# Forty-eight weight tiles in a 512-column matmul form: GLU, part of the first MLP product, and the end of the scan's input and the keys

## The chip, the cores and the metric

The kernel runs on one core of one Trainium2 chip. The metric is the device time of one execution in microseconds (us). Before the change it is 1356.16 us, the median of 3 runs (1355.76 to 1356.31). "Within 0.2%" means within 2.7 us of that.

Engines are named as the profile names them: PE is TensorE's matmuls and PEld its weight loads, DVE is VectorE, ACT is ScalarE, POOL is GpSimd, SP is SyncE, whose queue issues most of the transfers.

## The reference

One decoder block, 256 positions of width 2048, everything in float32. A condition vector c makes six modulation rows (adaLN). A first norm and modulation give h. One product with `w_in` gives the input u of a state-space scan, the queries, keys and values of attention, and two gates. The two branches are gated, merged, projected and added to x; a second norm and modulation give h2, and an MLP with squared ReLU follows.

```python
c_act = jax.nn.silu(c)
mod = c_act @ w_ada[l] + b_ada[l]
h = rms_norm(x, norm_mix_g[l]) * (1.0 + sc1) + sh1
proj = h @ w_in[l]
u, q, k, v, ga, gb = jnp.split(proj, split_at, axis=-1)
...
    y = jax.nn.gelu(y).astype(u.dtype)
    return y * jax.nn.sigmoid(y @ w_glu + b_glu)
...
merged = (jax.nn.sigmoid(ga) * (y_ssm @ w_proj_ssm[l])
          + jax.nn.sigmoid(gb) * (y_att @ w_proj_attn[l]))
x = x + g1 * (merged @ w_out[l])
h2 = rms_norm(x, norm_mlp_g[l]) * (1.0 + sc2) + sh2
x = x + g2 * (jnp.square(jax.nn.relu(h2 @ w_ff1[l])) @ w_ff2[l])
return rms_norm(x, norm_final_g)
```

## The kernel before

**Products in three parts.** TensorE multiplies in a reduced float32 format (float32r). To keep the precision, every operand is split into a high part (rounded to float32r) and a low part (what is left), and a product is the sum of high x high, high x low and low x high. `split` (L179) does this for a weight tile: ACT casts `wraw` to `whi`, DVE subtracts to get `wlo`.

**Weight tiles.** All big products stream their weights through `stream` (L190) in tiles `wraw` of 128 partitions x 1024 columns (512 KB). There are seven buffers of `wraw` and four each of `whi` and `wlo`. A tile is either one row tile (128 rows) by 1024 columns or, where `kts` is given in pairs, two row tiles by 512 columns (`load`, L170).

**Three forms of a product.**

- `steps_t` (the "pt" form; `gemm_t` runs it): the weights are the stationary operand, h the moving one, and the result comes out transposed (columns of the weights on the partitions). For one weight tile it issues, for each of eight blocks of 128 columns, three matmuls of 256 columns (L270 high x high, L271 high x low, L272 low x high): 24 matmuls and 24 weight loads.
- `gemm_d` (the "pd" form, L279): the same product, but the high and the low part of h lie side by side, so that one matmul of 512 columns does high x high and high x low at once (L289), into the two halves of a PSUM bank; a matmul of 256 columns adds low x high to the second half (L293). A tile (two row tiles by 512 columns) has four blocks and two row tiles: 8 matmuls of 512 and 8 of 256 columns. The two halves of the bank have to be added when it is emptied. The result of one call is 512 columns wide, so 1024 columns take two calls ("halves" here, h = 0 and 1).
- `steps_n` (the "pn" form; `gemm_n`): h is stationary, the weights move, 12 matmuls of 512 columns for each tile (L327, L329, L331).

**PSUM banks.** `four` (L113) gives a product its four banks. As long as `turn` is None it takes them in turn from five ("mm"), so that a product finds one bank free and three that the product before has to release. From the MLP's second part on (`turn` is set to False at its start) products alternate between two sets. Three more banks ("ax") serve the small matmuls. `seeded` (L232) refills the banks with a partial sum before a product that continues an earlier one: one ACT copy for each bank, after the last cast of a weight tile emitted so far (`wcast`).

**Order.** Each engine runs its instructions in an order fixed when the program is built, by a planner that simulates the engines and takes what is ready by priority; loads and splits of weight tiles and the refills have a raised priority. `after(x)` adds an order behind instruction x.

**Lanes.** Between weight tiles, `step` runs small jobs from lanes. A lane has a rate: so many jobs for each tile. The lane "ada" makes the adaLN rows: each job loads a 512 KB tile of `w_ada` and multiplies and sums it on DVE (L391) one tile later. Its rate is set stage by stage by the constants R1 to R5, RS0 to RS3, RPA, RWO and RM. What is left of all lanes after the first part of the MLP is run at once by `flush` (L1677). The last jobs of that lane make the modulation of the last row tiles of h2. The lane "ssm" builds the scan's parameters on DVE.

**Stages.** The rows of h become ready in groups of 1, 3, 4 and 8 row tiles, so q, k, v, u and the first gate are computed in pieces that continue one another (`qkvu`; `duo` interleaves two). The last pieces come in this order: first gate and q interleaved, u (row tiles 8 to 15, L1337, about 186 to 212 us), `hop_in` (u is moved to another layout by 32 small transfers on POOL's queue), k (L1340, to 239 us), v (to 265 us; attention starts in it), then the rest of the gates beside attention and the scan. Then come one half of the attention projection, GLU (L1412, 451.5 to 474.6 us), the other half, the scan's projection, the merge, `w_out`, and the MLP.

**The MLP's first product** begins before all of h2 is known: for four units of 1024 columns (NP = 4) the row tiles that are ready are multiplied first and put into `part`. Unit 0 has four row tiles; units 1 to 3 have eight each (L1656, 647 to 718.5 us). `ff1` later adds the remaining row tiles with `gemm_d`.

## Time and profile before

| | us |
|---|---|
| median of 3 runs | 1356.16 |
| lowest, highest | 1355.76, 1356.31 |
| profiled execution | 1356.04 |
| its span, first to last instruction | 1354.3 |
| PE busy | 1342.8 |
| DVE busy | 1038.2 |
| ACT busy | 751.1 |
| POOL busy | 49.0 |

The profile is of one execution. Its page gives for each engine the busy time, a row of 40 equal slices of the span with the busy share in tenths, the clock granted to TensorE, the transfers, the chain of waits that ended last, and the costliest groups of instructions. A group line reads: source line, engine, operation, what it writes from what it reads, shapes, count, then busy us, the mean duration of one in ns, and the idle time of the engine before them with what ended it. A timeline line reads: start in us, duration in us, engine, source line, operation, and, in brackets, idle time of the engine before it. A line of the chain in order of time reads: start, duration, instruction, how many. A line of windows gives, for a stretch of the span, the busy time of each engine with the number of instructions, TensorE's granted clock, the busy share of the transfer engines, and GB/s. A matmul's duration runs from its start to its modelled end, and matmuls overlap.

### The profile page before, as it was taken

What the parts mean: (1) busy time and instruction counts of PE and PEld (TensorE: products, weight loads), DVE (VectorE), ACT (ScalarE), POOL (GpSimd) and SP (SyncE); (2) the same over time, 40 slices, a digit from 0 to 9 for tenths busy, and PEclk for the clock granted to TensorE, in tenths of its full rate; (3) what the DMA queues carried; (4) which work ended last, traced back from release to release, by engine and by line L of the source; (5) the groups of instructions that cost most, each with busy time, mean ns of one, the idle gap of its engine ahead of it and who ended that gap; (6) DMA issues with size and microseconds to landing.
All of it is one profiled execution on the core that took longest, in us unless ns stands there. A gap on an engine that the chain in (4) does not pass through costs nothing.

```text
span 1354.3 us, 21608 instructions
## 1 busy us (share of the span) xinstructions
PE 1342.8 (99%) x8276; PEld 1167.6 (86%) x8276; DVE 1038.2 (77%) x1441; ACT 751.1 (55%) x1045; POOL 49.0 (4%) x105
## 2 busy tenths in 40 slices
PE   9999999999999999999999999999999999999997
PEld 8898899788888988888998888888888888888886
DVE  7888998677987888988888967686765555565687
ACT  7768656766558543455546656353554544535544
POOL 0000004200004000000000000000000000000000
PEclk9999999999999999999999999999999999999999
DMA  9999977975568888997899897888878666566552
GB/s 377 407 408 409 389 252 210 306 241 180 159 215 262 314 283 300 334 337 290 291 342 339 296 235 263 220 281 258 276 243 230 190 187 197 187 188 198 176 196 83
DMA packets 116856, 357.09 MB, mean 264 GB/s; under 512 B 16728, under 2 KB 16864, under 8 KB 116464
## 3 DMA queue, kind: packets, MB, share of 16 engines
q1 hardware_dynamic: 113056, 348.83, 76.5%
q0 software_dynamic: 3120, 5.70, 1.4%
q8 instruction: 65, 1.06, 0.3%
q10 hardware_dynamic: 576, 1.18, 0.3%
q14 instruction: 39, 0.32, 0.1%
HBM read 350.79 MB, written 2.51 MB: 261 GB/s over the span
## 4 chain that ended last, share of the span: by engine, by line
PE 95%; ACT 2%; DMA 2%; DVE 1%; issue 0%; SPq 0%; ACTq 0%; DVEq 0%
PE pn L327 18%; PE pn L329 18%; PE pn L331 18%; PE pd L289 14%; PE pd L293 7%; PE pt L270 6%; PE pt L272 6%; PE pt L271 6%; DMA wraw<-in_w_in_dram 1%; PE ys L992 1%; ACT whi L184 1%; DMA xt<-in_xt_dram 0%; PE trh L834 0%; PE vr L954 0%; PE rk L794 0%
## 5 line engine op out<-in xcount | busy, mean ns | idle before, releaser
L186 DVE TENSOR_TENSOR wlo<-wraw,whi 128x1024 fp32r<-128x1024 f32 x448 | 546.2, 1224 | 254.4 <-ACT whi L184 253.0
L184 ACT CAST whi<-wraw 128x1024 fp32r<-128x1024 f32 (+1 forms) x449 | 467.3, 1051 | 479.6 <-PE pn L329 214.3
L289 PE MATMUL pd<-h2h,whi 128*128 128x512 f32 x800 | 207.3, 393 | 0.2 <-ACT whi L184 0.2
L327 PE MATMUL pn<-whi,ff 128*128 128x512 f32 x496 | 193.3, 390 | 0.0
L329 PE MATMUL pn<-whi,ff 128*128 128x512 f32 x496 | 193.3, 390 | 0.0
L331 PE MATMUL pn<-wlo,ff 128*128 128x512 f32 x496 | 190.9, 390 | 0.0
L289 PEld LDWEIGHTS pd<-h2h,whi 128*128 128x128 f32 x800 | 141.3, 189 | 22.9 <-ACT whi L184 0.4
L391 DVE SCALAR_TENSOR_TENSOR wraw<-wraw,cb 128x1024 f32<-128x1024 f32 x128 | 156.2, 1221 | 0.0
L327 PE MATMUL pn<-whi,ah 128*128 128x512 f32 x320 | 126.7, 400 | 0.8 <-ACT qk L1216 0.4
L329 PE MATMUL pn<-whi,ah 128*128 128x512 f32 x320 | 125.5, 392 | 0.0
L293 PEld LDWEIGHTS pd<-h2h,wlo 128*128 128x128 f32 x800 | 114.8, 190 | 11.5
L293 PE MATMUL pd<-h2h,wlo 128*128 128x256 f32 x800 | 117.9, 282 | 0.0
L331 PE MATMUL pn<-wlo,ah 128*128 128x512 f32 x320 | 115.9, 392 | 0.4 <-DVE wlo L186 0.4
L331 PEld LDWEIGHTS pn<-wlo,ff 128*128 128x128 f32 x496 | 93.1, 188 | 19.5
L329 PEld LDWEIGHTS pn<-whi,ff 128*128 128x128 f32 x496 | 93.2, 188 | 19.0
L327 PEld LDWEIGHTS pn<-whi,ff 128*128 128x128 f32 x496 | 93.1, 188 | 19.1
L270 PE MATMUL pt<-ah,whi 128*128 128x256 f32 x384 | 105.9, 286 | 0.2 <-DVE tz L611 0.2
L271 PE MATMUL pt<-ah,whi 128*128 128x256 f32 x384 | 104.9, 283 | 0.0
L272 PE MATMUL pt<-ah,wlo 128*128 128x256 f32 x384 | 95.9, 284 | 0.8 <-DVE wlo L186 0.7
L270 PEld LDWEIGHTS pt<-ah,whi 128*128 128x128 f32 x384 | 73.4, 192 | 1.8 <-ACT whi L184 0.7
L271 PEld LDWEIGHTS pt<-ah,whi 128*128 128x128 f32 x384 | 73.4, 192 | 0.2
L327 PEld LDWEIGHTS pn<-whi,ah 128*128 128x128 f32 x320 | 59.9, 188 | 15.3 <-ACT whi L184 1.3
(386 smaller groups left out, 2009.3 us busy)
## 6 DMA issues: line engine op xcount, KB each, us to landing
wraw<-in_w_ff_dram SPq DMA_DIRECT2D x256, 512.0 KB, 4.8
wraw<-in_w_in_dram SPq DMA_DIRECT2D x128, 512.0 KB, 6.1
wraw<-in_wat_dram SPq DMA_DIRECT2D x128, 512.0 KB, 5.9
ahm<-in_wat_dram SPq DMA_DIRECT2D x48, 512.0 KB, 10.2
wraw<-in_w_out_dram SPq DMA_DIRECT2D x32, 512.0 KB, 6.5
wraw<-in_w_proj_attn_dram SPq DMA_DIRECT2D x16, 512.0 KB, 5.7
wraw<-in_w_proj_ssm_dram SPq DMA_DIRECT2D x16, 512.0 KB, 6.4
ahm<-in_wan_dram SPq DMA_DIRECT2D x8, 512.0 KB, 10.6
```

Of the source, the lines that this page charges most:

```text
L184: h = self.nc.scalar.copy(hi[:, c], src[:, c])
L186: s = self.nc.vector.tensor_sub(lo, src, hi.bitcast(F32))
L270: nc.tensor.matmul(o, hi[:, c], xh[:, kx, :], start=st, stop=False, skip_group_check=True)
L271: nc.tensor.matmul(o, hi[:, c], xl[:, kx, :], start=False, stop=False, skip_group_check=True)
L272: self.mm = nc.tensor.matmul(o, lo[:, c], xh[:, kx, :], start=False, stop=sp, skip_group_check=True)
L289: nc.tensor.matmul(banks[blk], hi[:, cut(blk, k)], x2[:, ks[k], :, :], start=i + k == 0, stop=False, skip_group_check=True)
L293: self.mm = nc.tensor.matmul(banks[blk][:, S:2 * S], lo[:, cut(blk, k)], x2[:, ks[k], 0, :], start=False, stop=last and k == 1, skip_group ...
L327: nc.tensor.matmul(o, xh[:, kx, tk], hi[:, c], start=q == 0 and not full, stop=False, skip_group_check=full)
L329: nc.tensor.matmul(o, xl[:, kx, tk], hi[:, c], start=False, stop=False, skip_group_check=full)
L331: self.mm = last = nc.tensor.matmul(o, xh[:, kx, tk], lo[:, c], start=False, stop=q == n - 1, skip_group_check=full)
L391: v.scalar_tensor_tensor(w, w, 1.0, self.cb[:, (i % 2) * 1024:(i % 2 + 1) * 1024], op0=OP.mult, op1=OP.mult, accum_out=pc[:, i:i + 1])
L992: nc.tensor.matmul(p[q, c], self.cc[q, i, j].rearrange("p s c -> p (s c)"), self.sri[q, b % 2, i, c], start=i == 0, stop=False)
```

## The change

It moves 48 weight tiles from the pt form to the pd form: u's and k's last eight row tiles (8 tiles each), GLU (8) and units 1 to 3 of the MLP's first part (24). Each product of 1024 columns becomes two halves of 512.

- `gemm_d` takes a `seed`. The partial sum goes into the first half of each bank, and the second half is filled with zeros (ACT copies of the new column `zero`); the first matmul then accumulates.
- `join` empties a bank: ACT copies the second half, DVE adds the first half.
- `wide_last` replaces the last calls of `qkvu` for u and k. `duo` no longer prepares the first tile of u ahead (`prime`); v's is prepared in the second half of k.
- GLU: the split y lies as [row tile, high/low]; sigmoid, gating and split of the first four blocks follow the first half.
- The rates of the adaLN lane change in four places (R3, R4, RS0, RM).

```diff
-R3 = .25
-R4 = .7
+R3 = .15
+R4 = .8
 R5 = .9
-RS0 = .4
+RS0 = .55
...
-RM = 1.0
+RM = .8
...
-    def gemm_d(self, src, kts, c0, x2):
+    def gemm_d(self, src, kts, c0, x2, seed=None):
         nc = self.nc
         banks = self.four("pd")
+        full = self.seeded(banks, seed)
+        if full:
+            with self.tc.high_priority(offset=OFF), self.after(self.seedgate), self.after(self.wcast):
+                for o in banks:
+                    nc.scalar.copy(o[:, S:2 * S], self.zero.to_broadcast([P, S]))
...
-                nc.tensor.matmul(banks[blk], hi[:, cut(blk, k)], x2[:, ks[k], :, :], start=i + k == 0, stop=False,
+                nc.tensor.matmul(banks[blk], hi[:, cut(blk, k)], x2[:, ks[k], :, :], start=i + k == 0 and not full, stop=False,
                                  skip_group_check=True)
...
+    def join(self, banks, dests, view=lambda o: o):
+        for o, d in zip(banks, dests):
+            self.nc.scalar.copy(d, view(o[:, S:2 * S]))
+            self.nc.vector.tensor_add(d, d, view(o[:, 0:S]))
...
-        duo(order[12], order[13], (0,) * 8 + (1,) * 4 + (0,) * 4 + (1,) * 4, order[14])
-        qkvu(order[14])
+        duo(order[12], order[13], (0,) * 8 + (1,) * 4 + (0,) * 4 + (1,) * 4, None)
         self.want = lambda kt: None
+
+        def wide_last(which, after=None):
+            src, kts, c0 = place(which, 3, 3)
+            view = (lambda o: o.rearrange("p (c s) -> p s c", s=4)) if which == 3 else (lambda o: o)
+            for h in range(2):
+                dests = [self.uT[:, :, 4 * h + b, :] if which == 3 else self.qk[:, which, 4 * h + b, :] for b in range(4)]
+                seed = [lambda o, d=d: (view(o[:, 0:S]), d) for d in dests]
+                banks = self.gemm_d(src, kts, c0 + 512 * h, a2, seed)
+                if h and after:
+                    self.prime(*place(*after))
+                self.join(banks, dests, view)
+        wide_last(3)
         self.hop_in()
-        qkvu((1, 3, 3), (2, 3, 3))
+        wide_last(1, (2, 3, 3))
         self.lanes["ada"][1] = R4
...
-        yy = self.slot("VT", [P, 2, 8, S], F32R, name="yy")
+        yy = self.slot("VT", [P, 8, 2, S], F32R, name="yy")
...
-        banks = self.gemm_t(a["w_glu"][0], range(8), 0, yy[:, 0], yy[:, 1])
...
-        for b in range(4):
-            t = sg[:, b]
-            for k in range(2):
-                nc.scalar.activation(t[:, k], banks[b][:, k * S:(k + 1) * S], AF.Sigmoid,
-                                     bias=self.bglu[:, 2 * b + k:2 * b + k + 1])
-            s = slice(2 * b, 2 * b + 2)
-            v.tensor_mul(sc4(t), sc4(t), yT[:, s])
-            self.split(gg[:, 0, s], gg[:, 1, s], t)
+        for h in range(2):
+            banks = self.gemm_d(a["w_glu"][0], range(8), 512 * h, yy)
+            self.join(banks, [sg[:, 2 * h + b // 2, b % 2] for b in range(4)])
+            for b in (2 * h, 2 * h + 1):
+                t = sg[:, b]
+                for k in range(2):
+                    nc.scalar.activation(t[:, k], t[:, k], AF.Sigmoid, bias=self.bglu[:, 2 * b + k:2 * b + k + 1])
+                s = slice(2 * b, 2 * b + 2)
+                v.tensor_mul(sc4(t), sc4(t), yT[:, s])
+                self.split(gg[:, 0, s], gg[:, 1, s], t)
...
             if g:
-                banks = self.gemm_t(w1, range(0, 8), g * 1024, self.ah, self.al)
+                for h in range(2):
+                    self.join(self.gemm_d(w1, range(0, 8), g * 1024 + 512 * h, a2),
+                              [part[:, 2 * h + b // 2, (b % 2) * S:(b % 2 + 1) * S] for b in range(4)])
```

More of the change, by code (lines that the diff above doesn't have):

```diff
@@ L482, in consts @@
         nc.gpsimd.memset(self.mpos, MAGIC)
+        self.zero = self.col("zero", 1)
+        nc.gpsimd.memset(self.zero, 0.0)
         self.half = self.col("half", 1)
@@ L1318, in duo @@
             self.strict, self.seedgate = False, None
-            self.prime(*place(*after))
+            if after:
+                self.prime(*place(*after))
             evac(ub[0], banks[1], ub[1])
@@ L1335, in body @@
         qkvu(order[11], order[12], True)
-        duo(order[12], order[13], (0,) * 8 + (1,) * 4 + (0,) * 4 + (1,) * 4, order[14])
-        qkvu(order[14])
+        duo(order[12], order[13], (0,) * 8 + (1,) * 4 + (0,) * 4 + (1,) * 4, None)
         self.want = lambda kt: None
+        def wide_last(which, after=None):
[6 more added lines that the diff above has]
+                if h and after:
+                    self.prime(*place(*after))
+                self.join(banks, dests, view)
+        wide_last(3)
         self.hop_in()
-        qkvu((1, 3, 3), (2, 3, 3))
+        wide_last(1, (2, 3, 3))
         self.lanes["ada"][1] = R4
@@ L1408, in body @@
         for k in range(4):
-            self.split(sc4(yy[:, 0, 2 * k:2 * k + 2]), sc4(yy[:, 1, 2 * k:2 * k + 2]), yT[:, 2 * k:2 * k + 2])
+            self.split(sc4(yy[:, 2 * k:2 * k + 2, 0]), sc4(yy[:, 2 * k:2 * k + 2, 1]), yT[:, 2 * k:2 * k + 2])
         self.gate = self.hgate = None
         self.gates = [(None, None), self.done[-1]]
-        banks = self.gemm_t(a["w_glu"][0], range(8), 0, yy[:, 0], yy[:, 1])
         gg = self.slot("QT", [P, 2, 8, S], F32R, name="gg")
         sg = self.slot("S5", [P, 4, 2, S], name="sg")
-        for b in range(4):
-            t = sg[:, b]
-            for k in range(2):
-                nc.scalar.activation(t[:, k], banks[b][:, k * S:(k + 1) * S], AF.Sigmoid,
-                                     bias=self.bglu[:, 2 * b + k:2 * b + k + 1])
-            s = slice(2 * b, 2 * b + 2)
-            v.tensor_mul(sc4(t), sc4(t), yT[:, s])
-            self.split(gg[:, 0, s], gg[:, 1, s], t)
+        for h in range(2):
[8 more added lines that the diff above has]
+                self.split(gg[:, 0, s], gg[:, 1, s], t)
         proj_attn(1)
@@ L1556, in ff1 @@
                     else:
-                        nc.scalar.copy(q, banks[b][:, S:2 * S])
-                        v.tensor_add(q, q, banks[b][:, 0:S])
+                        self.join([banks[b]], [q])
                 self.flush("act")
@@ L1660, in body @@
                                     homes=[(wh[:, k, :], wl[:, k, :]) for k in range(4)])
-            for b in range(4):
-                if g:
-                    nc.scalar.copy(part[:, b, :], banks[b])
-                else:
+                for b in range(4):
                     with self.after(hs["h0"]):
```

## The prediction

> **What bounds the kernel now.** I read the profile's page first, then the chain of waits, then the timeline of the matmuls, because a busy matmul row says little about pace.
>
> ```profile
> span 1354.3 us, 21608 instructions
> PE 1342.8 (99%) x8276; PEld 1167.6 (86%) x8276; DVE 1038.2 (77%) x1441; ACT 751.1 (55%) x1045; POOL 49.0 (4%) x105
> PEclk9999999999999999999999999999999999999999
> PE 95%; ACT 2%; DMA 2%; DVE 1%; issue 0%; SPq 0%; ACTq 0%; DVEq 0%
> ```
>
> The chain that ended last is TensorE for 95% of the span, at full clock in every slice. So a stage gets shorter only where TensorE issues less work or issues it at a closer spacing. The profiled execution took 1356.04 us, 1.7 us more than its span and 0.1 us under the median of the runs shown (1356.16), so differences can be read against either.
>
> The groups give the old 256-column form and the new form's two parts these means:
>
> ```profile
> L270 PE MATMUL pt<-yy,whi 128*128 128x256 f32 x64 | 18.1, 283 | 0.0
> L289 PE MATMUL pd<-h2h,whi 128*128 128x512 f32 x800 | 207.3, 393 | 0.2 <-ACT whi L184 0.2
> L293 PE MATMUL pd<-h2h,wlo 128*128 128x256 f32 x800 | 117.9, 282 | 0.0
> ```
>
> By these means a weight tile (128 rows of 1024 columns) would cost 24 x 283 = 6.79 us in the old form (24 matmuls of 256 columns) and 8 x 393 + 8 x 282 = 5.40 us in the new one. That is a trap: the durations overlap. The timeline shows the starts. First and last matmuls of the GLU product (192 of them, old form), then three rows of the chain in order of time inside a later product that has the new form already:
>
> ```profile
> 451.52 0.28 PE L270 MATMUL pt<-yy,whi 128*128 128x256 f32 x1
> 451.64 0.28 PE L271 MATMUL pt<-yy,whi 128*128 128x256 f32 x1
> ...
> 474.56 0.40 PE L327 MATMUL pn<-whi,yh 128*128 128x512 f32 x1
> ```
>
> ```profile
> 952.88 1.84 PE pd L289 x8
> 954.72 0.95 PE pd L293 x8
> 955.67 1.84 PE pd L289 x8
> ```
>
> Old form: (474.56 - 451.52) / 192 = 0.120 us from start to start, so 24 x 0.120 = 2.88 us per weight tile. New form: 1.84 + 0.95 = 2.79 us per tile (0.230 per 512-column matmul, 0.119 per 256-column one). Both stream 6144 columns per tile; the new one saves eight matmul starts, and that is worth 0.09 us, not 1.4.
>
> **The change part by part.** *The saving.* Converted are 8 tiles of u, 8 of k, 8 of GLU and 24 of the MLP: 48 x 0.09 = 4.3 us of TensorE time, on the path everywhere.
>
> A page would make it less. The Trainium skill (TensorE: Matmul & The Clock Gate, section Back-to-back issue gap) gives N / 2.4 + 2.5 ns between matmuls of N columns; an estimate from that page is 2.62 us for an old tile and 2.60 for a new one, so 1.0 us for 48. The trace disagrees, with 2.88 and 2.79, and the sum goes by the trace.
>
> *Handing over the PSUM banks.* These products take four of five banks in turn. Today u, k, GLU and each MLP unit is one product; now each is two halves, so six hand-overs are new, and each finds one bank free and three that the half before has to release. In the last tile of a half a bank finishes every 0.70 us (2.79 / 4); the next half wants its banks 0.46 us apart (2 x 0.230). The fourth bank asked for was finished 0.70 us before the end and is wanted 1.38 us after it: 2.08 us. Emptying it now takes an ACT copy and a DVE add in place of one ACT copy; in u and k the refill with the earlier partial sum and a fill with zeros follow on ACT. Rows of the same shapes, and of DVE's usual work:
>
> ```profile
> L1557 ACT COPY fr<-pd 128x256 f32<-128x256 f32 x32 | 11.9, 373 | 10.0 <-PE pd L293 10.0
> L1558 DVE TENSOR_TENSOR fr<-fr,pd 128x256 f32<-128x256 f32 x32 | 13.2, 418 | 2.7 <-ACT fr L1557 1.9
> L237 ACT COPY pt<-qk 128x512 f32<-128x512 f32 x20 | 10.9, 601 | 0.0
> ...
> 703.30 1.22 DVE L186 TENSOR_TENSOR wlo<-wraw,whi 128x1024 fp32r<-128x1024 f32 x1
> 704.43 1.22 DVE L391 SCALAR_TENSOR_TENSOR wraw<-wraw,cb 128x1024 f32<-128x1024 f32 x1
> ```
>
> Without the refill: 0.37 + 0.42 = 0.79 us, plus whatever stands ahead on DVE, whose long pieces start 1.13 us apart. With one piece ahead it is 1.92 us, inside 2.08. With the refill (two more ACT pieces; the zero fill is shown nowhere, I bound it by 0.37 for a 256-column copy and 0.60 for a 512-column one, nearest the former) it is 0.79 + 0.74 + 1.13 = 2.66 us, 0.6 late. What such a hand-over costs TensorE today is seen where the last old-form MLP unit meets the first new-form product:
>
> ```profile
> 718.24 0.28 PE L272 MATMUL pt<-h2h,wlo 128*128 128x256 f32 x1
> 718.71 2.11 PE L289 MATMUL pd<-h2h,whi 128*128 128x512 f32 x8 [0.18 <-ACT whi L184]
> ...
> 949.95 1.98 PE L289 MATMUL pd<-h2h,whi 128*128 128x512 f32 x8
> ...
> 727.26 2.46 PE L289 MATMUL pd<-h2h,whi 128*128 128x512 f32 x10
> 729.56 0.40 PE L293 MATMUL pd<-h2h,wlo 128*128 128x256 f32 x2
> ```
>
> Its eight matmuls took 2.11 us, against 1.98 where banks are plentiful: 0.13 us. At 727.26 ten 512-column matmuls stand where a half's last tile has two before each pair of 256-column ones: eight of the following half were pulled ahead of a tile not ready yet: the order on TensorE is made round foreseeable waits, and the free bank offers 0.70 us of such work per tile in hand. I take 0.13 us for each of the six new hand-overs (0.8 us) and 0.15 us more for the three that refill (into u's second half and both halves of k): 0.45 us. Together 1.25 us; bounds are nothing and, with one long piece ahead everywhere, 3 x 0.6 + 0.8 = 2.6 us.
>
> *Vector and scalar work.* Added: 48 DVE adds, 48 ACT copies of 256 columns, and in u and k 16 refills and 16 zero fills in place of 8 refills of 512; 20 ACT copies of 512 go (4 each in u and k, 12 in the MLP; GLU's sigmoids read the banks themselves today). What is beside it:
>
> ```profile
> core 0: us, PE busy (x) PEld busy (x) DVE busy (x) ACT busy (x) POOL busy (x), PEclk, DMA share, GB/s
> 186.00:212.00 26.00, 26.00 (x365) 25.42 (x367) 23.62 (x28) 13.54 (x19) 0.00 (x0) 1.00 0.71 230
> 212.00:239.00 27.00, 27.00 (x311) 26.68 (x301) 23.85 (x29) 16.05 (x31) 17.97 (x37) 1.00 0.79 187
> 239.00:265.00 26.00, 26.00 (x125) 21.59 (x124) 15.64 (x27) 18.61 (x38) 5.84 (x11) 1.00 1.04 330
> 451.00:475.00 24.00, 24.00 (x198) 23.82 (x197) 20.65 (x29) 10.60 (x15) 0.00 (x0) 1.00 0.92 315
> 647.00:719.00 72.00, 71.82 (x600) 71.61 (x599) 60.63 (x88) 34.29 (x46) 0.00 (x0) 1.00 0.90 326
> ```
>
> In u and k (the first two rows) DVE has 47.5 us of work in 53. The 16 adds bring 5.3 to 6.7 (0.33 to 0.42 each, overlapped or not); R3 at .15 takes two adaLN pieces (1.22 each) out: 50.4 to 51.8 in 51.6 us. That is full. But the branch's parameter work in it isn't urgent, and the next stage has DVE at 15.64 of 26. Nothing, as long as the splits go first. GLU: 20.65 of 24 plus 2.6 to 3.4 is full too, with spill into the projection behind it. MLP: 60.6 - 5 x 1.22 + 24 x 0.33 to 0.42 = 62.4 to 64.6 of 69.9. ACT has room: 29.6 of 53 in u and k, and 48 x 0.37 - 16 x 0.60 = 8 more.
>
> *Rates and transfers.* I worked the adaLN lane's credits through tile by tile. In the last tiles of q, then u and k, it issues 3 jobs instead of 6; in v 7 instead of 5; in the first gate product 8 instead of 7; in the three MLP units 19 instead of 24, which leaves 5 for the flush behind them instead of 1. A job is 0.52 MB and 1.22 us of DVE. The third row is the tight one: transfers are full there (share 1.04), and one more job falls between k's last tile and v's last: 0.52 / 330 GB/s = 1.6 us. TensorE already starves there a little:
>
> ```profile
> 265.97 0.50 PE L327 MATMUL pn<-whi,ah 128*128 128x512 f32 x1 [0.29 <-ACT whi L184]
> 267.54 0.50 PE L331 MATMUL pn<-wlo,ah 128*128 128x512 f32 x1 [0.43 <-DVE wlo L186]
> ...
> L184 ACT CAST whi<-wraw 128x1024 fp32r<-128x1024 f32 x8 | 8.4, 1049 | 7.1 <-DMA wraw<-in_w_in_dram 5.5 <-PE pn L331 1.5
> ```
>
> I take nothing, since the code holds four split tiles ahead, with -0.7 us (these stalls gone) and +1.6 us as bounds. The four extra jobs of the flush are 4.9 us of DVE just before the last row tiles of h are needed, but five jobs fewer ran before them, so the sum of work ahead is the same: nothing, at most 4.9 less the 1.5 us that the order above leaves (727.26 to 729.1 is spent on other matmuls): 3.4 us. Weights now come as two row tiles of 512 columns; later products do so without starving: nothing. The new constant column on GpSimd: nothing. GLU's gating of its first four blocks moves beside the second half.
>
> **Sum.** -4.3 + 0.8 + 0.45 = -3.0 us: 1356.04 - 3.0 = 1353.0 us.
>
> **The rivals.** *A, no saving in the spacing.* Half a 512-column interval is 0.115 us, the lone 256-column one 0.119; if with h and yy the pair ran at 2 x 0.120, the 4.3 would go and 1.25 us stay: 1357.3. For it speaks the page's rule above, by which hardly anything is to be had; against it 800 matmuls at this pace on the same buffer layout. *B, the hand-overs take more.* One long DVE piece ahead everywhere and one more transfer late in v: -4.3 + 2.6 + 1.0 (between 0 and 1.6) = -0.7, 1355.3 us. For it: DVE is full in u, k and GLU. Against it: matmuls can be pulled forward. *C, slower, by DVE queueing before an add.* If not one but two long pieces stand ahead, the bank is released 0.79 + 2.26 = 3.05 us after it was finished, 1.0 late, and with a refill 1.7 late. Twelve hand-overs are open to it: the six new ones, and six that there are today but where the new form asks for its banks faster, or hands them on by an add (into GLU, from u to k, into each of the three MLP units, and behind the last of them). Three refill: 3 x 1.7 + 9 x 1.0 = 14 us, 1356.04 - 4.3 + 14 = 1365.8 if all are struck; half of them gives 1358.8. It decides from 7 us on, that is from half of them. For it: DVE in those stages is over 95% by the sums above. Against it: the hand-overs of today, beside a DVE at 85 to 90%, cost about 0.1 us each. *D, more than forecast:* free hand-overs and the v stalls gone: -4.3 - 0.7 = -5.0, 1351.0.
>
> **How the numbers follow.** About 0.2% (2.7 us) is what a measurement of this kernel can tell from no change. Forecast (1351.9 to 1354.2): 0.45. D: 0.12. B: 0.25. A: 0.05. C: 0.13. Of the forecast's 0.45 some 0.09 lies above 1353.4, within 0.2%. Faster by over 0.2%: 0.36 + 0.12 = 0.48; within: 0.09 + 0.25 + 0.05 = 0.39, slower 0.13. Range: from 1350.4 (D and its margin) to 1358.8 (half of C, over A and the late transfers).
>
> **What would show it.** Right: 512-column starts 0.230 us apart in u, k, GLU and MLP units; about 2.79 us per tile there; single gaps of some tenths of a us at the hand-overs. Wrong: spacing of 0.240 (A); TensorE waiting for the joining adds or for the refills by more than 0.5 us a time (B, C); waits for weight transfers in v, or for h's last row tiles after the flush. A result under 1350 would mean a stall in before that I have not seen.

## The result: 1.3% slower, and the profile after

| | before | after |
|---|---|---|
| median, same chip | 1356.24 us (4 runs, 1355.76 to 1358.42) | 1373.86 us (4 runs, 1371.93 to 1374.36) |
| ratio | | 1.0128, 95% interval 1.0113 to 1.0143 |
| profiled execution (span) | 1356.04 us (1354.3) | 1374.12 us (1372.3) |

The forecast was 1353.0 us and the range ended at 1358.8. From the page of after, in its order: span, engines, clock by slice, the chain that ended last, two groups.

```profile
span 1372.3 us, 20961 instructions
PE 1346.8 (98%) x7892; PEld 1147.2 (84%) x7892; DVE 1052.1 (77%) x1489; ACT 761.8 (56%) x1097; POOL 49.2 (4%) x106
PEclk9999999999999999999999999999999999999999
PE 86%; DVE 7%; ACT 3%; issue 2%; DMA 1%; DVEq 0%; ACTq 0%
L294 PE MATMUL pd<-h2h,whi 128*128 128x512 f32 x992 | 268.0, 394 | 3.8 <-ACT whi L184 2.5
L298 PE MATMUL pd<-h2h,wlo 128*128 128x256 f32 x992 | 156.1, 282 | 3.4 <-DVE wlo L186 3.4
```

384 matmuls fewer, and still TensorE is busy 4 us longer: a busy row says little about pace here as before. The chain tells more: TensorE held 95% of it, now 86%, and DVE went from 1% to 7%. The two groups now have idle time before them that ACT's casts and DVE's splits ended. To see in which stages the time went, I took the first matmul of each product from the timeline of after:

```profile
185.50 0.40 PE L294 MATMUL pd<-ah,whi 128*128 128x512 f32 x1
244.38 0.40 PE L337 MATMUL pn<-whi,ah 128*128 128x512 f32 x1
437.07 0.39 PE L337 MATMUL pn<-whi,yh 128*128 128x512 f32 x1
458.83 0.39 PE L294 MATMUL pd<-yy,whi 128*128 128x512 f32 x1
482.79 0.40 PE L337 MATMUL pn<-whi,yh 128*128 128x512 f32 x1
505.82 0.39 PE L337 MATMUL pn<-whi,gg 128*128 128x512 f32 x1
...
656.53 0.48 PE L294 MATMUL pd<-h2h,whi 128*128 128x512 f32 x1
792.72 0.40 PE L337 MATMUL pn<-whi,ff 128*128 128x512 f32 x1
```

In before, the starts that the prediction does not show (u, v, the first attention part, the scan's projection, the units, the product behind them):

```profile
185.80 0.28 PE L270 MATMUL pt<-ah,whi 128*128 128x256 f32 x1
238.81 0.48 PE L327 MATMUL pn<-whi,ah 128*128 128x512 f32 x1
429.76 0.39 PE L327 MATMUL pn<-whi,yh 128*128 128x512 f32 x1
496.34 0.39 PE L327 MATMUL pn<-whi,gg 128*128 128x512 f32 x1
647.02 0.36 PE L270 MATMUL pt<-h2h,whi 128*128 128x256 f32 x1
774.70 0.40 PE L327 MATMUL pn<-whi,ff 128*128 128x512 f32 x1
```

Differences of such starts give the stages:

| stage (first matmul to first matmul) | before | after |
|---|---|---|
| u and k | 53.02 | 58.88 |
| v and gates | 190.95 | 192.69 |
| GLU | 23.03 | 23.96 |
| second attention part of the projection | 21.79 | 23.03 |
| units 1 to 3 and the product behind them | 127.68 | 136.20 |

Together +18.3 us; the span is 18.0 longer, and all other stages agree within 0.3 us. Every edited stage lost, though by the saving alone each was to win 0.7 to 2.2 us.

What the units wait for, from the view of waits over 669 to 742 us (total, times, longest, us):

```profile
ACT whi L184 <- PE pd L294: 18.3, 3, 7.5
ACT whi L184 <- DMA wraw<-in_w_ff_dram: 16.1, 9, 9.6
DVE wlo L186 <- ACT whi L184: 11.9, 6, 3.8
PE pd L298 <- DVE wlo L186: 3.4, 6, 0.9
PE pd L294 <- ACT whi L184: 2.5, 3, 1.3
```

Read from below: TensorE waits for split weights, the splits for casts, and the casts for TensorE to let go of a buffer, or for loads that themselves were issued late. The four buffers of split weights come free late. The planned order of TensorE's built program (matmuls in a row on one bank and weight tile in one line, bank and tile numbers kept) says why:

```
2998 L294 MATMUL pd0_6752<-h2h_6464,whi_6758 128x512 x2
...
3003 L298 MATMUL pd0_6752<-h2h_6464,wlo_6759 128x256 x2
3004 L294 MATMUL pd0_6752<-h2h_6464,whi_6782 128x512 x2
...
3006 L294 MATMUL pd0_6752<-h2h_6464,whi_6807 128x512 x2
...
3008 L294 MATMUL pd0_6752<-h2h_6464,whi_6832 128x512 x2
3009 L294 MATMUL pd1_6753<-h2h_6464,whi_6758 128x512 x2
```

At a hand-over one bank of the five is free (6752). The planner fills it from all four weight tiles (6758, 6782, 6807, 6832) before the next bank is asked for. So every tile is held until the last bank has had it: four buffers fill together and come free together, and casts, splits and loads bunch behind them. This is the "0.70 us of such work per tile in hand" that the prediction counted as a protection.

### The profile page after: what moved, and what is told of

It reads as the page before. It is cut to its first block, busy times and chain, and to the rows that moved or that the text cites. A ratio compares the mean times of both kernels' runs of the same rounds, so it can differ in the third digit from the quotient of the medians.

```text
span 1372.3 us, 20961 instructions
## 1 busy us (share of the span) xinstructions
PE 1346.8 (98%) x7892; PEld 1147.2 (84%) x7892; DVE 1052.1 (77%) x1489; ACT 761.8 (56%) x1097; POOL 49.2 (4%) x106
## 4 chain that ended last, share of the span: by engine, by line
PE 86%; DVE 7%; ACT 3%; issue 2%; DMA 1%; DVEq 0%; ACTq 0%
PE pd L294 17%; PE pn L337 17%; PE pn L339 17%; PE pn L341 17%; PE pd L298 9%; PE pt L272 2%; PE pt L270 2%; PE pt L271 2%; DVE wraw L401 2%; DVE wlo L186 2%; DMA wraw<-in_w_ff_dram 1%; ACT whi L184 1%; ACT bp L776 1%; DVE rw L983 1%; PE rk L806 0%
## 5 line engine op out<-in xcount | busy, mean ns | idle before, releaser
L294 PE MATMUL pd<-h2h,whi 128*128 128x512 f32 x992 | 268.0, 394 | 3.8 <-ACT whi L184 2.5
L294 PEld LDWEIGHTS pd<-h2h,whi 128*128 128x128 f32 x992 | 170.7, 189 | 28.5 <-ACT whi L184 3.3
L298 PEld LDWEIGHTS pd<-h2h,wlo 128*128 128x128 f32 x992 | 149.4, 190 | 25.2 <-DVE wlo L186 6.5
L298 PE MATMUL pd<-h2h,wlo 128*128 128x256 f32 x992 | 156.1, 282 | 3.4 <-DVE wlo L186 3.4
L341 PE MATMUL pn<-wlo,ah 128*128 128x512 f32 x320 | 113.1, 396 | 2.0 <-DVE wlo L186 2.0
L337 PEld LDWEIGHTS pn<-whi,ah 128*128 128x128 f32 x320 | 60.3, 189 | 16.2 <-ACT v L1228 2.0
L341 PEld LDWEIGHTS pn<-wlo,ah 128*128 128x128 f32 x320 | 60.4, 189 | 14.8 <-DVE wlo L186 2.4
L339 PEld LDWEIGHTS pn<-whi,ah 128*128 128x128 f32 x320 | 60.4, 189 | 12.2
L270 PE MATMUL pt<-ah,whi 128*128 128x256 f32 x256 | 69.2, 285 | 0.2 <-DVE tz L623 0.2
L271 PE MATMUL pt<-ah,whi 128*128 128x256 f32 x256 | 68.7, 283 | 0.0
L272 PE MATMUL pt<-ah,wlo 128*128 128x256 f32 x256 | 60.2, 284 | 0.8 <-DVE wlo L186 0.7
```

Source lines behind the costliest of these rows:

```text
L270: nc.tensor.matmul(o, hi[:, c], xh[:, kx, :], start=st, stop=False, skip_group_check=True)
L271: nc.tensor.matmul(o, hi[:, c], xl[:, kx, :], start=False, stop=False, skip_group_check=True)
L272: self.mm = nc.tensor.matmul(o, lo[:, c], xh[:, kx, :], start=False, stop=sp, skip_group_check=True)
L294: nc.tensor.matmul(banks[blk], hi[:, cut(blk, k)], x2[:, ks[k], :, :], start=i + k == 0 and not full, stop=False, skip_group_check=True)
L298: self.mm = nc.tensor.matmul(banks[blk][:, S:2 * S], lo[:, cut(blk, k)], x2[:, ks[k], 0, :], start=False, stop=last and k == 1, skip_group ...
L337: nc.tensor.matmul(o, xh[:, kx, tk], hi[:, c], start=q == 0 and not full, stop=False, skip_group_check=full)
```

## The experiments

Stages as above ("u to gates" is u, k, v and gates; "GLU to scan" is GLU, the second attention part and the scan's projection, 45.43 in before), in us of the profiled execution. Where nothing is edited in "u to gates" and the rates are those of before, it still lies between 242.8 and 245.3, so differences of 1.5 us in that column are not read.

| run | median | ratio to before, 95% | u to gates | GLU to scan | units |
|---|---|---|---|---|---|
| before | 1355.75 to 1356.24 by job | 1 | 243.97 | 90.25 | 127.68 |
| after | 1373.86 | 1.0113 to 1.0143 | 251.57 | 92.42 | 136.20 |
| e1 units on two sets | 1366.68 | 1.0055 to 1.0088 | 251.61 | 93.17 | 129.75 |
| e2 old rates | 1372.92 | 1.0107 to 1.0137 | 249.69 | 92.81 | 136.23 |
| e3 new rates only | 1364.66 | 1.0046 to 1.0076 | 246.39 | 90.25 | 134.10 |
| e4 tile order | 1372.37 | 1.0102 to 1.0132 | 255.05 | 91.48 | 129.96 |
| e5 RM only | 1359.24 | 1.0016 to 1.0035 | 243.28 | 90.25 | 131.89 |
| e6 units alone, two sets | 1359.66 | 1.0019 to 1.0047 | 244.91 | 90.25 | 132.52 |
| e7 u and k alone | 1361.18 | 1.0023 to 1.0053 | 249.45 | 90.53 | 127.65 |
| e8 GLU alone | 1357.91 | 1.0007 to 1.0026 | 243.42 | 91.54 | 127.65 |
| e9 units mixed | 1356.19 | 0.9995 to 1.0013 | 243.27 | 90.25 | 129.00 |
| e10 units pinned | 1359.94 | 1.0019 to 1.0041 | 244.25 | 90.25 | 132.56 |
| e11 GLU, two sets | 1355.73 | 0.9989 to 1.0007 | 243.35 | 89.53 | 127.68 |
| e12 GLU and two units | 1355.23 | 0.9990 to 1.0007 | 242.82 | 89.53 | 126.74 |
| e13 u and k, no refill | 1358.91 | 1.0016 to 1.0036 | 246.74 | 90.25 | 127.66 |
| e14 the same, pinned | 1363.51 | 1.0039 to 1.0070 | 252.90 | 90.25 | 127.66 |
| e15 units, ACT release | 1358.50 | 1.0012 to 1.0034 | 244.48 | 90.25 | 128.40 |
| e16 the same, pinned | 1358.06 | 1.0009 to 1.0031 | 243.47 | 90.25 | 130.60 |
| e17 e16 and GLU | 1358.99 | 1.0014 to 1.0031 | 245.25 | 89.53 | 129.36 |

### Order, banks and rates: four changes to the pair

**e1**, after with the halves of the MLP units alternating between the two sets of PSUM banks:

```diff
                 self.lanes["ada"][1] = RM
                 self.agate = None
+                self.turn = False
```

> The changed kernel with one line more: from unit 1 of the MLP's first part on, the halves take their PSUM banks alternately from the two sets, so no half waits for the one before it. Theory O (order): with one free bank the planner runs a half block by block through all four of its weight tiles, so all four split buffers are needed at once and come free together; with banks at hand the order goes tile by tile, and the MLP units with the product behind them (656.5 to 792.9 us in the changed kernel, 136.4 us, against 127.8 before) shorten by 8 to 10 us: 1364 to 1366 us. Theory D (DVE load: 24 adds more and the splits late for that): the adds and the adaLN pieces stay, so the stretch stays within 2 us: 1372 to 1374. Theory R (the rates): the same as D.

**e2**, after with the four rates of before:

```diff
-R3 = .15
-R4 = .8
+R3 = .25
+R4 = .7
...
-RS0 = .55
+RS0 = .4
...
-RM = .8
+RM = 1.0
```

> The changed kernel with the four rates of before (R3 .25, R4 .7, RS0 .4, RM 1.0). Theory R: most of the loss is the rates, time 1358 or less. Theory O: the order block by block stays, so the converted stages stay long; only the single stalls in v (268.9 us) and beside the scan (377.2 us), 2 to 6 us with the clock's halving behind the latter, may go: 1367 to 1374. Theory D: more adaLN pieces in u, k and the MLP units on a DVE that is the bound: slower than the changed kernel, 1374 to 1380.

**e3**, before with the four rates of after (the diff reversed):

> The kernel of before with the four new rates alone. Theory R: slower by 3 us or more, with the stalls in v or beside the scan in it. Theories O and D: within 3 us of before (1353 to 1359), since no hand-over is new and DVE has no adds more.

**e4**, after with the matmuls of a weight tile ordered behind the last of the tile before, wherever halves share one set of banks:

```diff
+            turn = self.mm if i and self.turn is None else None
...
-                            f(blk, k)
+                            with self.after(turn):
+                                f(blk, k)
```

> The changed kernel, in which every matmul of a tile of a half is ordered behind the last matmul of the tile before it, wherever the banks come from one set (u, k, GLU, MLP units). The banks' hand-over, the adds, the rates are as in the changed kernel; only the order is tile by tile. Theory O in its strict form (the order does the harm, not the wait for the bank): the stalls of the converted stages fall from about 14 us to a few: 1360 to 1365. If the hand-over itself costs (each half waits 1 us for its banks): 1366 to 1372. Theory D: unchanged, 1372 to 1375.

Measured: in the units both e1 and e4 win back over 6 of the 8.5 us. In e1 no half waits for the banks of the half just before it; in e4 the banks are released as in after and only the order is forced. So in the units the order on the late banks makes most of the loss. Two rows for 669 to 700 us (busy time of PE, PEld, DVE, ACT, POOL, then the clock), after and e1:

```profile
669.00:700.00 31.00, 28.74 (x169) 24.39 (x168) 26.27 (x43) 15.65 (x28) 0.00 (x0) 1.00 0.89 306
```

```profile
669.00:700.00 31.00, 31.00 (x182) 27.32 (x181) 29.41 (x48) 15.67 (x25) 0.00 (x0) 1.00 1.00 361
```

With two sets TensorE does not pause in this stretch, DVE does 3 us more in the same time, and the same loads come at 361 GB/s instead of 306: DVE and the transfers were not full in after, they were waiting. What e1 still loses in the units it loses at their end, where transposes wait, as in e6 below. By its time e4 lies in theory D's range, but only because it loses in u and k what it wins in the units (66.36 us there, 58.88 in after): there the first matmuls of a half waited 5.13 us for the refilled bank, and the refill had waited for DVE's addition of the half before:

```profile
219.06 0.71 ACT L237 COPY pd<-qk 128x256 f32<-128x256 f32 x2 [5.54 <-DVE uT L313]
```

Undoing the rates changes the median by 0.9 us (e2), which the spread of the runs does not tell from nothing, yet alone they cost 8.7 us (e3, 1364.66 against 1355.96), 6.4 of them in the units. The loss of the rates and that of the form overlap; they do not add.

### The parts one by one, rates as in before

**e5**, before with one rate changed (the flush then holds five jobs; in before it holds one, not none as the expectation says):

```diff
-RM = 1.0
+RM = .8
```

> The kernel before with RM alone at .8, so that five adaLN jobs instead of none stand at the flush after the first MLP half's fourth unit; R3, R4 and RS0 stay. Theory F (the flush holds h's last row tiles back): the stages up to the MLP units as before (within 0.3 us each), units 1 to 3 with ff1(1,0) 131 to 134 us instead of 127.7 with the extra time between the flush and the first matmuls after it, the whole 1359 to 1362 us. Rival R (what the run with the new rates alone lost came of R3, R4 and RS0, which move jobs from v and the gates to later): units 127.7, the whole 1356 us.

**e6**, before with the units' part of the change alone and `self.turn = False` as in e1; **e7** with `wide_last` alone; **e8** with the GLU part alone (their diffs are the parts of the change's own).

> The kernel before with units 1 to 3 of the first MLP product in the 512-column form, their halves alternating between the two sets of PSUM banks; u, the keys, GLU and all rates as before. Theory O (the loss of the units comes of one free bank and an order block by block, and of the flush): with both gone the 24 tiles save 24 x 0.09 = 2.1 us: units and ff1(1,0) 125.2 to 126.2 us instead of 127.7, the whole 1353.5 to 1354.5 us. Rival Q (the form itself costs the units time, by its 32 DVE and ACT operations more): units 129 us or more, the whole 1357 us or more. Rival S (any new order costs some us somewhere): units 127.7 or less, but other stages longer.

> The kernel before with the last eight row tiles of u and the keys in the 512-column form and nothing else; rates as before. Theory U (the refills and zeroings by ACT and the sums by DVE come into a stretch in which both engines have the scan's setup to do; it costs by itself): u and k with v and the gates 248 to 252 us instead of 243.97, half-clock stretch near 240 us, the whole 1360 to 1364 us. Rival N (the loss there comes only with the other parts or the rates): 243.3 us, the whole 1355.5 us.

> The kernel before with GLU alone in the 512-column form; rates as before. Theory O: GLU 23.9 us instead of 23.03 and the second attention part of the projection 22.6 to 23.0 instead of 21.79, the whole 1357.7 to 1358.5 us. Rival N (those stalls come of what the other parts leave late): GLU 22.3 us, the projection 21.8, the whole 1355.5 us.

By its numbers e5 is as theory F expected: 4.2 us more in the units' stage, 1359.24 in all. The transposes of h's last row tiles (the tile view gives count, duration, first and last start) stand far ahead in before and at the very end in e5, before first:

```profile
L834 PE MATMUL trh<-ident,xs x13: 270/273/273, 694.2 to 707.7; 128*128 128x128 f32 x13
```

```profile
L834 PE MATMUL trh<-ident,xs x14: 272/273/328, 715.5 to 717.7; 128*128 128x128 f32 x14
```

In e5 TensorE had finished unit 3 by then and waited, 0.5 us between the transposes and 2.1 us for their results, and it ran at half clock for 3.4 us behind that (last section).

Theory F's reason does not hold, though. The column B of the modulation is the later of the two columns that a group of rows needs. It was done twice in this time, for row tiles 8 to 11 and for 12 to 15; before first, then e5:

```profile
675.16 0.16 DVE L1052 TENSOR_TENSOR B<-pcs,pack 128x4 f32<-128x4 f32 x1
...
720.02 0.16 DVE L1052 TENSOR_TENSOR B<-pcs,pack 128x4 f32<-128x4 f32 x1
```

```profile
677.08 0.16 DVE L1052 TENSOR_TENSOR B<-pcs,pack 128x4 f32<-128x4 f32 x1
...
714.66 0.16 DVE L1052 TENSOR_TENSOR B<-pcs,pack 128x4 f32<-128x4 f32 x1
```

By the order in the kernel, the first rows that TensorE waits for are 8 to 11. They had their columns 38 us before their transposes, and the last column came 5 us earlier in e5 than in before. So the flushed products did not hold the rows back; why the planner puts the transposes behind unit 3 with this rate is not shown.

e6 shows the same end with the old rates. Its unit 3 is through at 714.7 us, 3.5 us ahead of before, where most of these transposes are done by then; then TensorE waits (view of waits, 645 to 730 us):

```profile
PE pd L289 <- DVE h2h L186: 2.1, 1, 2.1
PE trh L839 <- ACT htmp L849: 1.3, 1, 1.3
```

It ran at half clock for 6.8 us behind these waits. Its times lie in rival Q's range (the form itself costs), but not for Q's reason: the loss is all at this end. The second set of banks has the three that the transposes use. Halves that alternate occupy it, so the transposes cannot be pulled forward; e9 below tests that. e8 has the forecast saving in GLU itself (22.35 us) and loses 2.0 us in the two stages behind it, by the bunching of after (view of waits, 455 to 480 us):

```profile
ACT whi L184 <- PE pd L289: 5.9, 4, 4.8
...
PE pn L336 <- DVE wlo L186: 0.9, 1, 0.9
```

e7 loses its time behind u and k, in v. Its pauses there, from the timeline of TensorE:

```profile
242.12 0.50 PE L341 MATMUL pn<-wlo,ah 128*128 128x512 f32 x1 [0.53 <-DVE wlo L186]
243.32 0.50 PE L337 MATMUL pn<-whi,ah 128*128 128x512 f32 x1 [0.70 <-ACT whi L184]
...
244.99 0.66 PE L770 MATMUL trv<-ident,bp 128*128 128x128 f32 x4 [0.94 <-ACT bp L776]
246.51 0.80 PE L872 MATMUL sco<-qk 128*128 128x128 f32 x2 [0.86 <-ACT bp L776]
```

Two wait for weights, two for ACT's copies of the scan's setup (`bp`), and from 246.2 to 249.6 us the clock is at a half. In after, u and k have the same sign: TensorE's only pauses over 0.1 us there, 0.87 and 1.20 us, wait for `bp` copies between which refills stand on ACT, with half clock from 233.4 to 236.8; none waits for a bank. On SP's queue, two loads of weights that stood 3.1 us apart in before (231.69 and 234.78) stand 5.8 apart in e7 (233.21 and 239.05), with six transfers of the scan between them instead of three. That alone does not make the loss: in e13 below they stand 8.9 apart (232.07 and 240.97), and its v and gates lose 0.9 us instead of 5.9.

Added up, 5.4 (e7) and 2.2 (e8) by medians and 8.6 for the units as they stand in e2 make 16.2 us, against 17.0 that e2 loses.

### Is it the hand-over, and which of its operations?

**e9**: e6 with e4's order, the last half of unit 3 on the first set. **e10**: all halves on the first set, with e4's order. **e11**: e8 with its two halves on the two sets.

```diff
                 for h in range(2):
+                    if g == 3 and h:
+                        self.turn = None
```

> The kernel before with units 1 to 3 in the 512-column form: halves alternate between the two sets of banks as in the run of the units alone, but the last half goes to the first set again (its weight tiles one after the other), so that the three other banks are free for the transposes of h's last rows during unit 3. Rates as before. Theory T (the run of the units alone gained its 2 us up to 715 us and lost 8 us after it because the transposes wait there for banks that its halves hold): units and ff1(1,0) 125.6 to 127 us instead of 127.7, the whole 1353.6 to 1355.2 us, no half clock. Rival W (the transposes are late because of DVE and ACT, which have the sums to do): a stall of 2 us or more between the transposes and the first matmuls on the last rows is left, half clock behind it, the whole 1358 us or more.

> The kernel before with units 1 to 3 in the 512-column form, all halves on the first set of banks, weight tiles one after the other, rates as before. Theory O (with the order tile by tile a hand-over costs only the wait for the sums of the half before): six hand-overs of 0.3 to 0.6 us against 2.1 us saved: 127.5 to 129 us, the whole 1355.5 to 1357.5 us, and no pile of waits for weight tiles inside a half. Rival (hand-overs as cheap as the prediction put them, 0.13 us each): 126.5 us, the whole 1354.6 us. Rival (the form on one set of banks loses whatever the order): 131 us or more, the whole 1359 us or more.

> The kernel before with GLU alone in the 512-column form, its two halves on the two sets of banks; rates as before. Theory O (the stalls behind GLU come of the order block by block, in which the four buffers of split weights come free together): GLU 22.3 us, the second attention part 21.8 instead of 23.0, the scan's projection 45.4 to 46.2, the whole 1355.0 to 1355.8 us. Rival (they come of the sums, sigmoids and splits that now stand in two portions among the weight splits on DVE and ACT): the projection keeps 23.0 and 46.2, the whole 1357 to 1358 us.

e11 settles GLU: 22.31 us (0.72 less, 8 tiles at 0.09), and nothing behind it is longer. e9 bears out theory T in that nothing waits for the transposes any more, but its units (129.00) are over T's range, since its one remaining hand-over stops TensorE for 1.9 us. e10 misses theory O by number and lies with the rival of 131 us or more: its first hand-over stops TensorE for 5.2 us, the other five for under 0.3 each. The timeline of e9 at the hand-over (DVE, ACT and TensorE rows):

```profile
704.56 0.92 ACT L307 COPY part<-pd 128x256 f32<-128x256 f32 x3
...
704.70 1.23 DVE L186 TENSOR_TENSOR wlo<-wraw,whi 128x1024 fp32r<-128x1024 f32 x1 [0.17 <-ACT whi L184]
...
705.84 1.22 DVE L398 SCALAR_TENSOR_TENSOR wraw<-wraw,cb 128x1024 f32<-128x1024 f32 x1
...
706.98 1.08 DVE L308 TENSOR_TENSOR part<-part,pd 128x256 f32<-128x256 f32 x3
...
707.46 0.74 PE L290 MATMUL pd<-h2h,whi 128*128 128x512 f32 x2 [1.91 <-DVE part L308]
```

The copies were done at 704.56 + 0.92 = 705.48; three additions stood behind one split and one adaLN product, and TensorE behind them. In e10 the split in front waited itself, for a cast, and the cast for a load:

```profile
660.14 1.04 ACT L184 CAST whi<-wraw 128x1024 fp32r<-128x1024 f32 x1 [3.83 <-DMA wraw<-in_w_ff_dram]
...
661.22 1.23 DVE L186 TENSOR_TENSOR wlo<-wraw,whi 128x1024 fp32r<-128x1024 f32 x1 [1.87 <-ACT whi L184]
...
663.50 1.41 DVE L308 TENSOR_TENSOR part<-part,pd 128x256 f32<-128x256 f32 x4
...
663.98 1.22 PE L290 MATMUL pd<-h2h,whi 128*128 128x512 f32 x2 [5.16 <-DVE part L308]
```

**e12** uses the form only where no half waits for sums: GLU as in e11, units 1 and 2 alternating, unit 3 in the old form. **e13** is e7 without refills and zeroing, **e14** the same with e4's order:

```diff
-                banks = self.gemm_d(src, kts, c0 + 512 * h, a2, seed)
+                banks = self.gemm_d(src, kts, c0 + 512 * h, a2)
...
-                self.join(banks, dests, view)
+                for o, d in zip(banks, dests):
+                    v.tensor_add(d, d, view(o[:, 0:S]))
+                    v.tensor_add(d, d, view(o[:, S:2 * S]))
```

> The kernel before with the 512-column form where no half has to wait for sums: GLU with its halves on the two sets of banks, units 1 and 2 of the first MLP product with halves alternating, unit 3 in the old form on the first set (the last half before it lies on the second), u and the keys in the old form, rates as before. Theory O: 24 tiles save their time whole: GLU 22.3 us (0.7 less), units and ff1(1,0) 126.2 to 126.6 us instead of 127.7 (16 x 0.09 = 1.4 less), nothing else longer, the whole 1353.8 to 1354.6 us, a ratio of 0.9985. Rival (a hand-over or the transposes of h's last rows stay late, as in the runs of the units): a stall of over 1 us near 700 or 716 us, the whole 1356 us or more.

> As the run of u and the keys alone, but without the refills and the zeroing: a half begins empty banks, and its two sums (high and low columns) are added to the partial sums in SBUF by two DVE additions per bank, in place of an ACT copy and one addition. 24 ACT operations less, 8 DVE operations more. Theory U (refills and zeroing on ACT make the loss there): u and k with v and the gates 244 to 246 us instead of 249.4, the whole 1356 to 1357.5 us. Theory O (the buffers of split weights come free together, so that loads are issued behind the block of 4.88 us on SP, and all that follows is late): 248 us or more, the whole 1360 us or more.

> The same, with the matmuls of a half ordered weight tile by weight tile. Theory O: with the order gone, what is left is the hand-over between the halves: u and k with v and the gates 244 to 245.5 us, the whole 1355.5 to 1357 us. Theory U (refills alone): as the run without the pinned order, within 0.5 us. Rival V (DVE's adaLN products and additions in one queue, as in the pinned units): one stall of 2 to 5 us at a hand-over between two halves, with half clock behind it, the whole 1360 us or more.

e12: GLU 0.72 and the units 0.94 us shorter, no pause over 0.7 us in the units, and a time that cannot be told from before (1355.23 against 1355.91). Its profiled execution took 1353.43, but 1.0 of that gain lies in stages that it doesn't edit. e13 and e14 split the loss of u and k: without refills (and without the joining copies on ACT) 2.7 of the 5.5 us are back, and of these about 1.7 are the half clock of e7, which e13 does not have. Of the rest 1.9 us lie in u and k, where again an addition hands over a bank. In e13:

```profile
224.87 2.35 DVE L735 TENSOR_TENSOR tt<-bp,AB 128x1024 f32<-128x1024 f32 x2
227.14 0.74 DVE L1361 TENSOR_TENSOR qk<-qk,pd 128x256 f32<-128x256 f32 x2
```

Two products of the scan's parameters stand in front, and TensorE waited 2.2 us. Pinning made it worse (e14: three such waits, 6.6 us, and 6.8 us at half clock), which neither theory O nor U had; rival V had it, with one such wait.

**e15** takes the addition off the release: one ACT copy of the bank's 512 columns into SBUF, where DVE adds the halves later. **e16** adds e4's order, **e17** GLU as in e11.

```diff
+                        for b in range(4):
+                            nc.scalar.copy(room[:, b], banks[b])
+                            v.tensor_add(dests[b], room[:, b, 0:S], room[:, b, S:2 * S])
```

> The kernel before with units 1 to 3 in the 512-column form on one set of banks, order left to the planner, but a bank is released by one ACT copy of all its 512 columns into SBUF, and DVE adds the two halves there later (only the last half of unit 3 keeps the addition from the bank). Rates as before. Theory A (the additions in DVE's queue hold the banks, and that is the whole loss): units and ff1(1,0) 126 to 127.5 us instead of 127.7, the whole 1354 to 1355.7 us. Theory O (the order block by block, which is still planned here, loses by itself, whoever releases the banks): waits for split weights inside the halves as in the kernel after, units 130 us or more, the whole 1358 us or more.

> The same with the weight tiles of a half one after the other. Theories A and O both: neither additions nor order are left, so that the 24 tiles keep most of 24 x 0.09 = 2.1 us: units and ff1(1,0) 125.6 to 126.8 us, the whole 1353.8 to 1355.2 us, no half clock. Rival (a release by ACT stands behind casts of weights that wait for their loads, as the additions stood behind splits): one hand-over of 2 to 5 us is left, the whole 1357 us or more.

> The same with GLU in the 512-column form on the two sets of banks as well: 0.7 us less than the run before it in every theory, by A and O 1353.1 to 1354.5 us, a ratio of 0.998 to 0.999; by the rival 1356 us or more.

In e15 TensorE does not pause inside the units (first row; columns as in the rows of e1):

```profile
645.00:717.00 72.00, 71.90 (x426) 63.08 (x424) 67.96 (x109) 40.48 (x58) 0.00 (x0) 1.00 0.91 322
717.00:725.00 8.00, 6.53 (x34) 4.94 (x32) 6.83 (x15) 6.60 (x12) 0.00 (x0) 1.00 1.02 389
```

But the expectation took for granted that the order would still be block by block, and it was not. In the built program of e15 a new half runs its first bank through three weight tiles at one hand-over (no pause over 0.1 us there) and through one or two at the others; in after it is all four each time. With banks that come free sooner the planner chose another order, so e15 changes release and order together and does not say which of the two would lose alone. What e15 still loses, it loses behind the units: 1.5 us idle between 717 and 725, where casts wait for weights. Its units (128.40) are 0.9 us over theory A's upper end and its median is in theory O's region; the profiled execution (1356.98) was one of the two fastest of seven, and where the slower ones lost more wasn't seen. e16 shows the rival: the release by ACT stands behind a cast that waits for its load, as the additions had:

```profile
659.58 1.04 ACT L184 CAST whi<-wraw 128x1024 fp32r<-128x1024 f32 x1 [3.46 <-DMA wraw<-in_w_ff_dram]
660.53 2.04 ACT L1674 COPY part<-pd 128x512 f32<-128x512 f32 x4
```

e17 has the same pause (2.5 us) and no gain, though every theory gave it 0.7 us. No version beat before by more than the measurement tells; e9, e11 and e12 are level with it.

## Why the prediction was wrong, step by step

- **The saving: right.** GLU in e11 goes from 23.03 to 22.31 us, 0.09 a tile; the starts in after are 0.23 us apart, as forecast.
- **Handing over the banks, 0.13 us each: the step that failed.** The working put one long DVE piece ahead (1.92 us, inside 2.08), and then set the price by one hand-over of before in which ACT releases the bank. Hand-overs by a DVE addition stopped TensorE for 1.9 (e9), 5.2 (e10), 2.2 (e13) and up to 3.3 us (e14) where pieces stood ahead, and for under 0.3 at the others of e10. What stands ahead has no bound of 1.13 us: a split waits for a cast, a cast for a load. Rival C named the queue and the addition, at a chance of 0.13; its price of at most 1.7 us a time was too low.
- **"Matmuls can be pulled forward": right as an observation, wrong as a protection.** The planner does it, and so holds all four weight tiles till the end of a half. In after the direct waits for an addition are short for that (0.3 to 0.6 us), but the weights come late: eleven pauses of 0.3 to 1.3 us between 669 and 742 us, 6.8 us in all. e4, which takes the order away and leaves the hand-overs, wins back 6.2 of the units' 8.5 us.
- **Refills, 0.45 us: mis-sized.** e7 against e13 gives up to 2.7 us, of which about 1.7 are the half clock; e13 also takes the joining copies off ACT. That they cost so much because they stand on ACT among the copies of the scan's setup fits the pauses of e7 and after, but no run has the refills alone. The zero fill's price was right (0.37 us).
- **DVE and ACT work at nothing, "as long as the splits go first": right in the sums, wrong in the condition.** DVE was not full in the units (61.7 of 73 us in after); the order in its queue decided. GLU's "spill into the projection" was named and priced at nothing; the 2.0 us that e8 loses there are not this spill, for e11 has the same DVE and ACT work and loses nothing. They are the hand-over on one set of banks.
- **Weights as two row tiles of 512 columns at nothing: right.** e1 loads them so at 361 GB/s, and TensorE does not pause from 669 to 700 us.
- **Rates and flush at nothing, at most 3.4 us: wrong.** e5 gives 4.2 us in the stage: the transposes came 21 us later, TensorE waited 2.7 us, and about 1.7 us went with the half clock. The term compared sums of DVE work and left the place of the transposes out. In after itself the rates cost the units nothing (136.20, with the old ones 136.23): its transposes run early (694 us), beside pauses that are there anyway.
- **Not in the prediction:** TensorE's clock falls to a half behind pauses (below), and the weights of a stage behind come late (e7, e15).

What stays open: why the weights come late behind u and k (e7) and behind the units (e15), why the rate moves the transposes (e5), and how much of after's loss up to the gates belongs to u and k and how much to the rates; the parts do not add there. So the cause is shown for GLU and the units, and only in part for u and k.

## What to carry to other kernels

Price a PSUM hand-over by everything that stands ahead of its last operation in a queue that is fixed beforehand, and ask what each of these pieces waits for; a saving of 0.09 us a tile is gone with one addition behind a split. Work that the planner can pull into a free bank is not free: it holds the buffers of all the tiles that it draws from. And a change of background work can cost without being late itself: look whether early work beside it, like the transposes of e5, keeps its place.

## What the runs showed of the hardware

The clock by slices looks full in after, yet the mean granted clock is 0.995 (0.999 in before). Short windows show why. Three of them around a pause in the gates (the last number but two of each row is the clock):

```profile
377.20:379.40 2.20, 0.43 (x2) 0.00 (x1) 2.20 (x3) 0.94 (x2) 0.00 (x0) 1.00 0.00 0
380.20:383.60 3.40, 3.40 (x10) 2.63 (x9) 3.40 (x5) 2.22 (x4) 0.00 (x0) 0.50 0.75 188
383.60:386.00 2.40, 2.40 (x39) 1.85 (x39) 2.37 (x4) 2.23 (x3) 0.00 (x0) 1.00 0.92 323
```

TensorE waits for a split in the first, and from 380.2 to 383.6 runs at half clock: its 512-column matmuls start 0.43 us apart instead of 0.23, and 1.7 us more are lost (an estimate, half of 3.4), just after the pause. In the page a slice is 34 us long, so 3.4 us at a half still show as a 9. After has two such stretches of 3.4 us. e5, e7, e9 and e16 have one of 3.4 us, e3, e6, e10 and e14 one of 6.8 us, e1, e2 and e4 two; before, e8, e11, e12, e13, e15 and e17 have none while products run. So part of most losses above is the clock: about 1.7 us in e5, e7 and e9, and about 3 us in e6.

The Trainium skill (TensorE: Matmul & The Clock Gate, section What's actually happening) puts the fall to half rate after at least one idle window of about 3.4 us, in windows that run freely. The stretches measured here are of that length, once and twice. What brings them on is less plain: a single pause of 1.9 to 2.4 us went ahead of it in after (at 377 us), e9 and e16, and in e10 and e16 the fall came while the pause still lasted; in e7 four pauses, none over 0.94 us, went with it (TensorE was busy for 2.48 of the 5.20 us before), and in after's first stretch the two of 0.87 and 1.20; but 2.2 us in e13 and 2.5 in e17 had none behind them. So a pause of 2 us can cost nearly twice its length, and whether it does could not be told beforehand.
